# A decoder layer on one core: chunk-wise loading of x, an unnormalised first feature that leaves PSUM at once, and the norm's root computed in one piece

## The chip, the cores and the metric

One Trainium2 chip; the program runs on one of its cores. Times are device microseconds of one execution of the program. A profiled execution is one execution taken with the hardware profiler; its span is the time from its first to its last recorded instruction.

## What is computed

One layer of a hybrid decoder in fp32 for 1,024 prompt tokens and 8 sample tokens (1,032 columns), model width 1,024. The token mix (sliding-window attention and a gated DeltaNet) is untouched by the change apart from the norm ahead of it. What matters here is the norm and the feed-forward part, which comes twice, and the norm at the end:

```python
def rmsnorm(x, g):
    y = x * lax.rsqrt(jnp.mean(x * x, axis=-1, keepdims=True) + EPS)
    return y * g

def swiglu(x, w_in, w_out):          # w_in: 1024 x 5632, w_out: 2816 x 1024
    gate, up = jnp.split(x @ w_in, 2, axis=-1)
    return (jax.nn.silu(gate) * up) @ w_out

x = x + 0.5 * swiglu(rmsnorm(x, ffn1_norm_g), ffn1_w_in, ffn1_w_out)
x = x + token_mix(rmsnorm(x, mix_norm_g), ...)
x = x + 0.5 * swiglu(rmsnorm(x, ffn2_norm_g), ffn2_w_in, ffn2_w_out)
y = rmsnorm(x, final_norm_g)
```

The norm is a factor for each token, so it may be applied before the product with `w_in` or behind it.

## The kernel before

**Layout.** x is held transposed: 8 tiles of 128 model rows, tokens along the free axis. In the feed-forward parts the 1,032 tokens are four chunks of 258 (`HW`), named by half p and place l in it (c = 2p + l). A block of x holds one chunk of one half of K (`kh`, four of the eight tiles: 128 x 1,032 numbers, 516 KB).

**Products.** fp32 operands are split into a rounded part `hi` and a rest `lo`; `mm3` (L318) makes three matmuls of each product: hi·hi (L321), hi·lo (L322), lo·hi (L323). Weights arrive as `r`, are cast by ScalarE to `phi` and split by VectorE to `plo`. Most of the feed-forward input product runs in a Strassen-like scheme (`ffn_in`, L651), with combined operands of weights (`wop`) and of x (`xhi`, `xlo`); these combine the two chunks of a half and both halves of K, and need x with its norm applied. They are built by `x_ops` (L441) on GpSimd, ScalarE and VectorE.

**The head.** So that TensorE has work before the norm is there, `ffn_head` (L614) makes the first features plainly: four in the first feed-forward part, three in the second (`HEAD`, L38). A feature is 128 of the 2,816 gate rows and the same up rows. It works on `xg` = x times the norm's gain only (`xghi` by ScalarE, `xglo` by VectorE; chunks in order, K tile by K tile, in the job `scale`, L1617). For each chunk, 24 matmuls go into a `ps` bank (gate) and 24 into an `mm` bank (up). There are five `ps` banks, in turn, and three `mm` banks. The result is evacuated by `evac` (L618): VectorE multiplies the gate bank by the row `rs` (the root, one for each token), ScalarE applies Silu, VectorE multiplies the up bank by `rs`, GpSimd multiplies the two, and SyncE stores 258 columns. An evacuation needs `rs` of its chunk; it waits in the list `due`, and `settle_rs` keeps at most two waiting for the first feature and one later.

**The norm.** `squares` (L771) squares the two blocks of a chunk on ScalarE, adds them on GpSimd and folds them twice on VectorE into `acc`. `rstd` (L360) sums over partitions with six narrow matmuls (L243), computes the root in twelve VectorE instructions on 86 x 6 numbers (`nv`, `rsqt`, `rsqy`), and then for each of its two chunks: three diagonal matrices (`ident` times a column of the root, in a temporary `t2`), three matmuls that broadcast them over partitions into a `ps` bank, and `use` (in `prepare`, L784): a ScalarE copy to `rs` and eight VectorE multiplications of x. The norms of the mix and of the end use `rstd` as well, with three chunks of 344 tokens, together or one by one.

**What sets the order.** TensorE executes in the order in which the program writes instructions (`ORDERED`, L43). Background jobs (the generators that are spawned: `scale`, `prepare`, weight casts, the norms) are advanced while the matmuls are written: each `yield` gives a planned time, in nanoseconds of TensorE work, by which the job is put off, `PAD` being 400. So a job's matmuls fall between those of the foreground. The order of VectorE, ScalarE, GpSimd and SyncE is set by a scheduler that simulates the engines; each engine then runs its list strictly in order. Buffers come from an arena of 44 slots; the temporaries `t2` have four buffers.

**The start.** `build` (L1594) loads the norm's gains, issues 12 warming matmuls on a tile of ones (L145), loads the first gate weights, then the four blocks of half 0 (by `kh`, then l), the first up weights, the four blocks of half 1 and the constants.

Of the kernel before, what the change touches and what calls it, by code (L numbers as in the profile page):

```python
# [13 lines left out]
AF = mybir.ActivationFunctionType  # L14
ALU = mybir.AluOpType
# [4 lines left out]
P = 128  # L20
D = 1024
# [22 lines left out]
ATT_GENS = 4  # L44
PAD = 400.0
KEEP = 2
WARM = 12
A_LIVE = 9
PAD_MERGE = 4000.0
DIRECT = 2  # L50
# [64 lines left out]
class Net:  # L115
# [244 lines left out]
    def rstd(self, acc, cs, use):  # L360
        nc = self.nc
        yield PAD
        m = 115 if cs[0][1] > HW else 86
        offs = [[c0, c0 + m, c0 + w - m] for c0, w in cs]
        n = 3 * len(cs)
        ps = self.pps()
        v = self.t("nv", [P, 12])
        for i, o in enumerate(sum(offs, [])):
            self.mmul(ps[:m, i:i + 1], acc[:, o:o + m], self.ones[:, 0:1])
        nc.vector.tensor_scalar(v[:m, :n], ps[:m, :n], 1.0 / D, EPS, ALU.mult, ALU.add)  # L370
        r = self.rsqrt(v[:m, :n])
        for j, (c0, w) in enumerate(cs):
            dgt = self.t2(3 * m)
            for i in range(3):
                nc.vector.tensor_scalar(dgt[:m, i * m:(i + 1) * m], self.ident[:m, :m], r[:, 3 * j + i:3 * j + i + 1], None, ALU.mult)
            yield PAD
            bcs = self.pps()
            for i, o in enumerate(offs[j]):
                self.mmul(bcs[:, o - c0:o - c0 + m], self.ones[:m, :], dgt[:m, i * m:(i + 1) * m])
            use(bcs, c0, w)  # L380

    def norm(self, x, gi, c0, w, acc, out):
        nc = self.nc
# [230 lines left out]
    def ffn_head(self, xg, rs, done, hd, head):  # L614

        nc = self.nc

        def evac(f, c, pg, pu):  # L618
            s = slice(c * HW, (c + 1) * HW)
            sg, h = self.t2(HW), self.t2(HW)  # L620
            nc.vector.tensor_tensor(sg, pg, rs[:, s], ALU.mult)
            nc.scalar.activation(sg, sg, AF.Silu)
            nc.vector.tensor_tensor(h, pu, rs[:, s], ALU.mult)
            nc.gpsimd.tensor_tensor(h, h, sg, ALU.mult)
            nc.sync.dma_start(hd[:, f, s], h)

        for f in range(head):
            ws = self.need_op(self.wops[f], 0)
            for c in range(4):
                p, l = divmod(c, 2)  # L630
                self.settle_rs(2)
                ps = self.pps()[:, :HW], self.pmm()[:, :HW]
                for o, (whi, wlo) in zip(ps, ws):
                    for k in range(KT):
                        while (k, c) not in xg["ready"]:
                            self.spin()
                        hi, lo = xg["t"][p][k // 4][l]
                        q, ks = slice(k % 4 * HW, (k % 4 + 1) * HW), slice(k * P, (k + 1) * P)
                        self.mm3(o, whi[:, ks], wlo[:, ks], hi[:, q], lo[:, q], k == 0, k == KT - 1)
                    if c == 3:  # L640
                        self.fr(whi, wlo)
                self.due.append((lambda p=p, l=l: (p, l) in done, partial(evac, f, c, *ps)))
                self.settle_rs(2 if f == 0 else 1)
                if f == head - 1:
                    self.fr(*xg["t"][p][0][l], *xg["t"][p][1][l])
                self.adv(2)
            self.wops[f].clear()
        self.settle_rs(0)
        self.fr(rs)

    def ffn_in(self, xT, hd, tail, head):  # L651
# [104 lines left out]
        self.split(hi, lo, raw, eng)  # L756
        return hi, lo

    def x_blocks(self, get, p):

        xs = []
        for kh in range(2):
            xs.append([])
            for l in range(2):
                b = self.bt([P, 4 * HW], s="x")
                c0 = (2 * p + l) * HW
                self.nc.sync.dma_start(b.rearrange("p (k c) -> p k c", k=4), get(kh, c0))
                xs[-1].append(b)
        return xs

    def squares(self, xs, acc):  # L771

        nc = self.nc
        for l in range(2):
            yield from self.need(2)
            a, b = self.bt([P, 4 * HW], s="sq"), self.bt([P, 4 * HW], s="sq")
            nc.scalar.activation(a, xs[0][l], AF.Square)
            nc.scalar.activation(b, xs[1][l], AF.Square)
            nc.gpsimd.tensor_tensor(a, a, b, ALU.add)
            nc.vector.tensor_tensor(a[:, :2 * HW], a[:, :2 * HW], a[:, 2 * HW:], ALU.add)  # L780
            nc.vector.tensor_tensor(acc[:, l * HW:(l + 1) * HW], a[:, :HW], a[:, HW:2 * HW], ALU.add)
            self.fr(a, b)

    def prepare(self, p, xs, acc, gi, out, rs, done, sq=None):  # L784

        nc = self.nc
        if sq is not None:
            while any((KT - 1, 2 * p + l) not in sq for l in range(2)):
                yield -300.0
            yield from self.squares(xs, acc)  # L790

        def use(bcs, c0, w):
            l = c0 // HW
            nc.scalar.copy(rs[:, (2 * p + l) * HW:(2 * p + l + 1) * HW], bcs[:, :w])
            done.add((p, l))
            for k in range(KT):
                y = xs[k // 4][l][:, k % 4 * HW:(k % 4 + 1) * HW]
                nc.vector.scalar_tensor_tensor(y, y, self.norm_g[:, gi, k:k + 1], bcs[:, :w], ALU.mult, ALU.mult)

        yield from self.rstd(acc, [(0, HW), (HW, HW)], use)  # L800
        self.fr(acc)
        for ok in self.x_ops([xs[0][0], xs[0][1], xs[1][0], xs[1][1]], 4 * HW, out):
            yield -300.0 if ok else -500.0
# [790 lines left out]
def build(tc, io):  # L1594
    with ExitStack() as ctx:
        ctx.enter_context(tc.manual_schedule(engines=ORDERED))
        n = Net(tc, ctx, io)
        nc = tc.nc
# [61 lines left out]
        xT = [[], []]  # L1660
# [98 lines left out]
```

## Time and profile before

| what | us |
|---|---|
| median of three runs | 2114.11 |
| lowest and highest of them | 2110.12 to 2117.31 |
| profiled execution | 2115.43 |
| its span | 2113.2 |
| TensorE busy in it | 2024.6 |
| mean granted TensorE clock | 0.973 of full |

The first feed-forward part's head lies in the first 142 us of the span, the second's between about 1375 and 1470; the final norm ends the span. In the rows of the profile an instruction that a helper records has the helper's line (L89 for VectorE, ScalarE and GpSimd, L102 for SyncE), so there one goes by tile names: `xghi`/`xglo` are the splits of x times gain, `phi`/`plo` those of weights, `sq` and `acc` the squares, `nv`, `rsqt`, `rsqy` the root, `t<-ident` a diagonal, `x<-x,c_norm_g,ps` the norm's multiplication, `t<-ps,rs` and `t<-mm,rs` the evacuation, `sw` the result of `ffn_in`. Lengths of neighbouring instructions of an engine overlap by a little, so a chain is better read from start to start. A granted clock of 0.50 means that matmuls stream at half speed.

### The profile page before, as it was taken

Reading aid. Unit: us, or ns where it says so; the run is one execution under the profiler, and the core shown is the slowest. Engines: PE = TensorE matmul, PEld = TensorE weight load, DVE = VectorE, ACT = ScalarE, POOL = GpSimd, SP = SyncE. Lnnn points to the kernel's source line nnn. Section 1 sums busy time; section 2 is a strip of 40 time slices with the busy share of each in tenths; the row PEclk is TensorE's granted clock in tenths of the full one; section 3 lists DMA queues with packets and bytes.
Section 4 is the critical chain, followed back from the end, with each engine's and each line's share of the span. In section 5 each row is a group of like instructions: output and inputs, shape, how many; then the busy total and the mean of one; then the engine's idle time right before and its main releaser. Section 6 shows DMA issues by size and latency. Waiting matters only on the chain.

```text
span 2113.2 us, 37138 instructions
## 1 busy us (share of the span) xinstructions
PE 2024.6 (96%) x15062; PEld 1963.6 (93%) x15062; DVE 1222.1 (58%) x2624; ACT 699.8 (33%) x1491; POOL 594.9 (28%) x517
## 2 busy tenths in 40 slices
PE   7799999999999999999999979999999999999997
PEld 6799999999999998787888869899999999999997
DVE  7755555555533544676977874685555555464335
ACT  5233333333211333545243332443333333331112
POOL 3354444341000131332211111245444444200003
PEclk7999999999999999999999979999999999999999
DMA  4112222227322221211212151221222222552112
GB/s 152 60 58 91 81 73 84 86 71 281 113 68 60 84 81 35 69 45 32 67 46 50 57 181 35 97 70 61 86 81 83 79 81 76 194 195 84 55 41 81
DMA packets 109771, 180.81 MB, mean 86 GB/s; under 512 B 35168, under 2 KB 63744, under 8 KB 109584
## 3 DMA queue, kind: packets, MB, share of 16 engines
q1 hardware_dynamic: 109568, 178.41, 26.6%
q8 instruction: 118, 1.93, 0.4%
q14 instruction: 53, 0.43, 0.1%
q0 software_dynamic: 32, 0.03, 0.0%
HBM read 135.60 MB, written 43.85 MB: 85 GB/s over the span
## 4 chain that ended last, share of the span: by engine, by line
PE 40%; DVE 8%; DMA 1%; issue 1%; SPq 1%; ACT 0%; POOL 0%; DVEq 0%; ACTq 0%; POOLq 0%
PE mm L321 6%; PE mm L322 6%; PE mm L323 6%; PE ps L528 4%; PE ps L530 4%; PE ps L529 4%; PE ps L243 3%; PE mm L528 2%; PE mm L530 2%; PE mm L529 2%; DVE conv L89 1%; DVE inv L89 1%; SPq L102 1%; DVE Tb L89 1%; DVE x L89 1%
## 5 line engine op out<-in xcount | busy, mean ns | idle before, releaser
L528 PE MATMUL ps<-xhi,wop 128*128 128x258 f32 x1480 | 421.0, 284 | 7.4 <-DVE sw L89 7.2
L530 PE MATMUL ps<-xhi,wop 128*128 128x258 f32 x1480 | 419.3, 283 | 0.0
L529 PE MATMUL ps<-xlo,wop 128*128 128x258 f32 x1480 | 419.3, 283 | 0.0
L321 PE MATMUL mm<-hhi,hi 128*128 128x344 f32 x1008 | 322.3, 320 | 0.0
L322 PE MATMUL mm<-hlo,hi 128*128 128x344 f32 x1008 | 322.3, 320 | 0.0
L323 PE MATMUL mm<-hhi,lo 128*128 128x344 f32 x1008 | 321.6, 319 | 0.0
L89 DVE TENSOR_TENSOR wop<-r,wop 128x512 fp32r<-128x512 f32 x185 | 158.5, 859 | 253.9 <-ACT wop L89 239.8
L528 PEld LDWEIGHTS ps<-xhi,wop 128*128 128x128 f32 x1480 | 280.9, 190 | 8.7 <-issue 7.2
L529 PEld LDWEIGHTS ps<-xlo,wop 128*128 128x128 f32 x1480 | 281.9, 191 | 0.0
L530 PEld LDWEIGHTS ps<-xhi,wop 128*128 128x128 f32 x1480 | 281.2, 190 | 0.0
L89 DVE SCALAR_TENSOR_TENSOR x<-mm,x 128x344 f32<-128x344 f32 x240 | 123.3, 515 | 220.0 <-PE mm L323 217.9
L89 ACT CAST hi<-raw 128x1024 fp32r<-128x1024 f32 (+1 forms) x78 | 76.7, 984 | 357.0 <-PE mm L322 327.0
L321 PEld LDWEIGHTS mm<-hhi,hi 128*128 128x128 f32 x1008 | 189.4, 188 | 0.3 <-DVE x L89 0.3
L323 PEld LDWEIGHTS mm<-hhi,lo 128*128 128x128 f32 x1008 | 189.4, 188 | 0.0
L322 PEld LDWEIGHTS mm<-hlo,hi 128*128 128x128 f32 x1008 | 189.3, 188 | 0.0
L89 POOL TENSOR_TENSOR acc<-acc,t 128x344 f32<-128x344 f32 (+1 forms) x50 | 45.5, 911 | 508.2 <-ACT t L89 495.9
L321 PE MATMUL mm<-xnhi,hi 128*128 128x344 f32 x488 | 172.1, 353 | 0.0
L528 PE MATMUL mm<-xhi,wop 128*128 128x258 f32 x592 | 167.5, 283 | 0.0
L530 PE MATMUL mm<-xhi,wop 128*128 128x258 f32 x592 | 167.2, 283 | 0.0
L529 PE MATMUL mm<-xlo,wop 128*128 128x258 f32 x592 | 167.0, 282 | 0.0
L89 ACT CAST wop<-r 128x512 fp32r<-128x512 f32 x185 | 114.7, 621 | 144.6 <-PE mm L530 77.0
L323 PE MATMUL mm<-xnhi,lo 128*128 128x344 f32 x488 | 158.6, 325 | 0.0
(320 smaller groups left out, 4607.5 us busy)
## 6 DMA issues: line engine op xcount, KB each, us to landing
r<-in_w_in SPq DMA_DIRECT2D x86, 512.0 KB, 3.6
hraw<-hd SPq DMA_DIRECT2D x44, 516.0 KB, 5.0
hd<-sw SPq DMA_DIRECT2D x74, 258.0 KB, 2.0
raw<-in_w_out SPq DMA_DIRECT2D x34, 512.0 KB, 4.0
raw<-in_w_mix SPq DMA_DIRECT2D x22, 512.0 KB, 3.6
raw<-in_w_out SPq DMA_DIRECT2D x24, 384.0 KB, 3.2
x<-in_x SPq DMA_DIRECT2D x16, 516.0 KB, 9.0
xd<-x SPq DMA_DIRECT2D x24, 172.0 KB, 1.9
```

Of the source, the lines that this page charges most:

```text
L89: return fn(out, *a, **k)
L102: return self.eng.dma_start(out, src)
L243: self.nc.tensor.matmul(out, lhsT, rhs, start=start, stop=stop)
L321: mm(ps, whi, xhi, start=start, stop=False)
L322: mm(ps, whi, xlo, start=False, stop=False)
L323: mm(ps, wlo, xhi, start=False, stop=stop)
L528: mm(ps, w[:, a], x[0][:, c], start=first, stop=False, skip_group_check=True)
L529: mm(ps, w[:, a], x[1][:, c], start=False, stop=False, skip_group_check=True)
L530: mm(ps, wlo, x[0][:, c], start=False, stop=last, skip_group_check=True)
```

## The change

- There are 18 warming matmuls in place of 12.
- x is loaded chunk by chunk in half 0: both blocks of chunk 0, then the up weights, then both blocks of chunk 1, then half 1.
- The addition of two squared blocks runs on VectorE in half 0 of the first head; in half 1 it stays on GpSimd.
- Feature 0 of a head no longer waits for the root: two ScalarE copies for each chunk take gate and up from PSUM into two tiles `early` of 1,032 columns. When all four chunks of `rs` are there, a job multiplies both tiles by `rs` on VectorE, applies Silu on ScalarE, multiplies on GpSimd and stores the feature with one DMA in place of four. `settle_rs` keeps one evacuation waiting in the other features, as before.
- In `rstd`, the root and the first chunk's diagonals are emitted at high priority; then the job yields 2,500 (`PAD_B`) in place of 400 before the first broadcast. The diagonals of the next chunk are emitted at high priority right behind the broadcast of the one before, into a tile `dgt` that has a single buffer, and a yield of 400 follows each `use`. Both heads, the norm of the mix and that at the end are affected.

TensorE's list has the same length otherwise, and its matmuls the same shapes.

```diff
-WARM = 12
+WARM = 18
+PAD_B = 2500.0
...
-        nc.vector.tensor_scalar(v[:m, :n], ps[:m, :n], 1.0 / D, EPS, ALU.mult, ALU.add)
-        r = self.rsqrt(v[:m, :n])
+
+        def diag(j):
+            d = self.t("dgt", [P, 345], bufs=1)[:, :3 * m]
+            for i in range(3):
+                nc.vector.tensor_scalar(d[:m, i * m:(i + 1) * m], self.ident[:m, :m], r[:, 3 * j + i:3 * j + i + 1], None, ALU.mult)
+            dgts.append(d)
+
+        dgts = []
+        with self.tc.high_priority():
+            nc.vector.tensor_scalar(v[:m, :n], ps[:m, :n], 1.0 / D, EPS, ALU.mult, ALU.add)
+            r = self.rsqrt(v[:m, :n])
+            diag(0)
+        yield PAD_B
         for j, (c0, w) in enumerate(cs):
-            dgt = self.t2(3 * m)
-            for i in range(3):
-                nc.vector.tensor_scalar(dgt[:m, i * m:(i + 1) * m], self.ident[:m, :m], r[:, 3 * j + i:3 * j + i + 1], None, ALU.mult)
-            yield PAD
+            dgt = dgts[j]
             bcs = self.pps()
             for i, o in enumerate(offs[j]):
                 self.mmul(bcs[:, o - c0:o - c0 + m], self.ones[:m, :], dgt[:m, i * m:(i + 1) * m])
+            if j + 1 < len(cs):
+                with self.tc.high_priority():
+                    diag(j + 1)
             use(bcs, c0, w)
+            yield PAD
...
+        def first():
+            while len(done) < 4:
+                yield -300.0
+            for t in early:
+                nc.vector.tensor_tensor(t, t, rs, ALU.mult)
+            nc.scalar.activation(early[0], early[0], AF.Silu)
+            nc.gpsimd.tensor_tensor(early[1], early[1], early[0], ALU.mult)
+            nc.sync.dma_start(hd[:, 0, :], early[1])
+            self.fr(*early)
+            yield PAD
+
+        early = [self.bt(s="early") for _ in range(2)]
         for f in range(head):
...
-                self.due.append((lambda p=p, l=l: (p, l) in done, partial(evac, f, c, *ps)))
-                self.settle_rs(2 if f == 0 else 1)
+                if f:
+                    self.due.append((lambda p=p, l=l: (p, l) in done, partial(evac, f, c, *ps)))
+                    self.settle_rs(1)
+                else:
+                    for t, o in zip(early, ps):
+                        nc.scalar.copy(t[:, c * HW:(c + 1) * HW], o)
...
+            if f == 0:
+                late = self.spawn(first())
             self.wops[f].clear()
         self.settle_rs(0)
+        self.wait(late)
         self.fr(rs)
...
-    def x_blocks(self, get, p):
-
-        xs = []
-        for kh in range(2):
-            xs.append([])
-            for l in range(2):
+    def x_blocks(self, get, p, xs=None, ls=(0, 1)):
+
+        xs = [[], []] if xs is None else xs
+        for l in ls:
+            for kh in range(2):
...
-            nc.gpsimd.tensor_tensor(a, a, b, ALU.add)
+            eng.tensor_tensor(a, a, b, ALU.add)
...
-        xs = [n.x_blocks(src(io["x"]), 0)]
+        xs = [n.x_blocks(src(io["x"]), 0, None, (0,))]
         n.adv()
+        n.x_blocks(src(io["x"]), 0, xs[0], (1,))
         xs.append(n.x_blocks(src(io["x"]), 1))
...
-            n.spawn(n.prepare(p, xs[p], n.bt(s="acc"), 0, xT[p], rs, done, xg["ready"]))
+            n.spawn(n.prepare(p, xs[p], n.bt(s="acc"), 0, xT[p], rs, done, xg["ready"], (n.nc.vector, n.nc.gpsimd)[p]))
```

More of the change, by code (lines that the diff above doesn't have):

```diff
@@ L767, in x_blocks, with squares @@
                 self.nc.sync.dma_start(b.rearrange("p (k c) -> p k c", k=4), get(kh, c0))
-                xs[-1].append(b)
+                xs[kh].append(b)
         return xs
-    def squares(self, xs, acc):
+    def squares(self, xs, acc, eng):
         nc = self.nc
@@ L782, in squares, with prepare @@
             self.fr(a, b)
-    def prepare(self, p, xs, acc, gi, out, rs, done, sq=None):
+    def prepare(self, p, xs, acc, gi, out, rs, done, sq=None, eng=None):
         nc = self.nc
@@ L789, in prepare @@
                 yield -300.0
-            yield from self.squares(xs, acc)
+            yield from self.squares(xs, acc, eng)
         def use(bcs, c0, w):
```

## The prediction

> **What bounds the kernel now.** The first part of the page says which engine fills the span.
>
> ```profile
> PE 2024.6 (96%) x15062; PEld 1963.6 (93%) x15062; DVE 1222.1 (58%) x2624; ACT 699.8 (33%) x1491; POOL 594.9 (28%) x517
> ```
>
> TensorE is idle for only 2113.2 - 2024.6 = 88.6 us, so a change that leaves the products alone, as this one does, can win only idle time and time at a low clock. Where these lie is read from the table by stretches; after the stretch and its length stand busy time and count of PE, PEld, DVE, ACT and POOL, then the granted clock, DMA share and GB/s.
>
> ```profile
> 0.00:20.00 20.00, 11.79 (x50) 10.22 (x50) 10.36 (x18) 14.48 (x28) 5.23 (x9) 0.69 0.89 287
> 20.00:40.00 20.00, 16.69 (x123) 16.69 (x123) 17.69 (x33) 11.89 (x22) 10.13 (x3) 0.80 0.31 107
> 40.00:60.00 20.00, 14.35 (x106) 14.04 (x105) 16.54 (x52) 5.50 (x8) 4.41 (x3) 0.83 0.11 34
> 60.00:80.00 20.00, 11.59 (x67) 11.50 (x68) 19.83 (x31) 6.25 (x10) 11.11 (x5) 0.74 0.13 39
> 80.00:120.00 40.00, 40.00 (x336) 40.00 (x335) 14.09 (x26) 7.46 (x13) 8.23 (x9) 1.00 0.23 68
> 120.00:160.00 40.00, 36.84 (x293) 36.46 (x292) 25.37 (x31) 16.04 (x26) 27.11 (x18) 0.96 0.20 63
> 900.00:1100.00 200.00, 190.82 (x1377) 168.73 (x1376) 151.18 (x458) 92.62 (x276) 46.76 (x45) 0.95 0.18 47
> 1100.00:1300.00 200.00, 177.46 (x1370) 165.31 (x1369) 146.73 (x504) 69.35 (x194) 31.70 (x15) 0.92 0.29 84
> ```
>
> The first 80 us hold 25.6 us of idle TensorE (8.21 + 3.31 + 5.65 + 8.41) and a clock of 0.69 to 0.83; from 80 on it is full: 336 products in 40 us, 0.119 us each. This is the head that the change rewrites. The DeltaNet stage (900 to 1300) idles 31.7 us and is not the target. The longest waits of TensorE in the first 150 us say for whom (sum, times, longest):
>
> ```profile
> PE mm L321 <- DVE t L89: 7.8, 1, 7.8
> PE ps L321 <- ACT xghi L89: 5.1, 2, 3.2
> PE ps L321 <- DVE x L89: 3.5, 1, 3.5
> PE mm L323 <- DVE plo L89: 3.4, 1, 3.4
> PE ps L528 <- DVE sw L89: 3.0, 1, 3.0
> ```
>
> The timeline of TensorE gives the places (start, length, instruction, idle before and releaser).
>
> ```profile
> 8.75 0.58 PE L321 MATMUL ps<-xghi,phi 128*128 128x258 f32 x1 [3.21 <-ACT xghi L89]
> 23.31 0.58 PE L323 MATMUL mm<-xghi,plo 128*128 128x258 f32 x1 [3.43 <-DVE plo L89]
> 43.53 1.55 PE L243 MATMUL ps<-t,ones 86*128 86x86 f32 x6 [2.81 <-DVE t L89]
> 53.44 0.80 PE L243 MATMUL ps<-t,ones 86*128 86x86 f32 x6
> 64.91 0.55 PE L321 MATMUL mm<-xghi,phi 128*128 128x258 f32 x1 [7.76 <-DVE t L89]
> 74.77 0.36 PE L321 MATMUL ps<-xghi,phi 128*128 128x258 f32 x1 [3.49 <-DVE x L89]
> 93.64 0.28 PE L321 MATMUL ps<-xghi,phi 128*128 128x258 f32 x1
> ```
>
> Feature 0 (8 groups of 24 products) runs from 8.75 to 53.4, feature 1 from there to 93.64, where feature 2 starts; behind that TensorE stays full but for one 3.0 us wait, so time won before 93.64 is carried to the end.
>
> **Feature 0: loads, early evacuation, squares.** The SyncE queue at the start (x are blocks of tokens, r raw weights: the first r is the gate, the second the up half), before and then after:
>
> ```order
> L102 DMA r_2_91<-in_w_in1 128x512 x2
> L102 DMA x_5_100<-in_x 128x4x258
> L102 DMA x_6_102<-in_x 128x4x258
> L102 DMA x_7_104<-in_x 128x4x258
> L102 DMA x_8_106<-in_x 128x4x258
> L102 DMA r_9_108<-in_w_in1 128x512 x2
> ```
> ```order
> L103 DMA r_2_97<-in_w_in1 128x512 x2
> L103 DMA x_5_106<-in_x 128x4x258
> L103 DMA x_6_108<-in_x 128x4x258
> L103 DMA r_7_110<-in_w_in1 128x512 x2
> L103 DMA x_10_119<-in_x 128x4x258
> L103 DMA x_11_121<-in_x 128x4x258
> ```
>
> The up weights pass two blocks of x, and the second block is now the other half of chunk 0, not the first half of chunk 1. ScalarE casts in that order; its rows, and VectorE's and GpSimd's beside them:
>
> ```profile
> 8.18 1.71 ACT L89 ACTIVATE xghi<-x,c_norm_g 128x258 fp32r<-128x258 f32 x4 [2.74 <-DMA x<-in_x]
> 9.80 1.05 ACT L89 ACTIVATE sq<-x 128x1032 f32<-128x1032 f32 x1
> 18.43 1.12 ACT L89 CAST phi<-r 128x512 fp32r<-128x512 f32 x2
> 45.12 0.38 ACT L89 COPY rs<-ps 128x258 f32<-128x258 f32 x1 [8.90 <-PE ps L243]
> ```
> ```profile
> 16.40 5.65 DVE L89 SCALAR_TENSOR_TENSOR xglo<-x,c_norm_g,xghi 128x258 fp32r<-128x258 f32 x4 [0.87 <-ACT xghi L89]
> 22.57 0.68 DVE L89 TENSOR_TENSOR plo<-r,phi 128x512 fp32r<-128x512 f32 x1
> ```
> ```profile
> 16.05 2.39 POOL L89 TENSOR_TENSOR sq<-sq,sq 128x1032 f32<-128x1032 f32 x1 [13.63 <-ACT sq L89]
> 18.60 2.37 POOL L89 TENSOR_TENSOR sq<-sq,sq 128x1032 f32<-128x1032 f32 x1 [0.17 <-ACT sq L89]
> ```
>
> Start to start, a block takes ScalarE 9.80 - 8.18 = 1.62 us, so neighbours overlap by 0.09; a square counts 0.95, a cast of half a weight tile 0.56, a copy 0.34. The order after the change, from 8.18: block 9.8, square 10.75, block 12.4, square 13.3, two casts 14.4. So chunk 0's gate products end near 14.2 and, with two splits of 0.68 on VectorE, its up products can start at 15.8 instead of 19.1 to 23.3. At half clock they end at 20.9, at full clock at 18.7. From 14.4 ScalarE goes on with chunk 1 (two blocks, two squares, one copy: 19.9, its second block done at 19.0), chunk 2 (second block 24.1), chunk 3 (27.7): TensorE follows by one chunk, gate of c3 done at 31.0, the norm's sums 32.0, c3's up products (24 x 0.119 = 2.9) at 34.9. It was 53.4: **-18.4 us**, the largest term. The eight copies cost 8 x 0.34 = 2.7 us of ScalarE, counted in; each waits for products that are done when it comes up, so nothing behind it is held.
>
> The two adds of squares that go from GpSimd to VectorE: VectorE's group of four splits took 5.65 us where GpSimd added (16.05 to 20.97). The adds on VectorE I count at 1.2 us each, twice the 0.6 of a 512-column split, which is less than the 5.65 shows lost to GpSimd.
>
> The six extra warming products end near 7.8 us and leave about 1 us idle where 3.2 stood. I do not count on a full clock (the 48 products of 8.75 to 28.0 all ran at 0.50), since c1 waits for ScalarE anyway; it is worth at most 1.5 us, in the low end.
>
> **Feature 1: broadcasts and the root.** Old cost: 93.6 - 53.4 = 40.2. VectorE and GpSimd at its largest wait (57 to 65):
>
> ```profile
> 41.35 0.16 DVE L89 TENSOR_TENSOR rsqt<-rsqy 86x6 f32<-86x6 f32 x1
> 59.17 2.23 DVE L89 SCALAR_TENSOR_TENSOR rsqy<-rsqt,rsqy 86x6 f32<-86x6 f32 x1
> 61.43 2.67 DVE L89 TENSOR_SCALAR t<-ident,rsqy 86x86 f32<-86x86 f32 x3
> 71.39 3.23 DVE L89 SCALAR_TENSOR_TENSOR x<-x,c_norm_g,ps 128x258 f32<-128x258 f32 x8
> ```
> ```profile
> 59.00 2.37 POOL L89 TENSOR_TENSOR t<-x,t 128x1032 f32<-128x1032 f32 x1
> 61.34 2.35 POOL L89 TENSOR_TENSOR x<-x,x 128x1032 f32<-128x1032 f32 x1
> ```
>
> A 6-column step of the root, 0.16 us alone, took 2.23 us and ended with the GpSimd add beside it, while the x multiplications, which read PSUM, ran at 3.23 / 8. The Trainium skill, "SBUF — State Buffer", section "Who interferes with whom", says the same: a VectorE instruction with two SBUF inputs waits out a GpSimd instruction that reads SBUF, one with a single SBUF input does not. By it each such root step can cost up to one GpSimd add; if nothing were waited out, the wait below would be 2.8 us shorter.
>
> The places of root and diagonal on VectorE (t2 or dgt from ident are the diagonals of a chunk's root, the x rows its normalisation), before:
>
> ```order
> L89 SCALAR_TENSOR_TENSOR x_8_106<-x_8_106,c_norm_g_74,ps_71_561 128x258 x4
> L89 TENSOR_TENSOR rsqt_69_539<-rsqy_68_538 86x6
> L89 SCALAR_TENSOR_TENSOR rsqt_69_539<-rsqt_69_539,nv_67_530 86x6
> L89 SCALAR_TENSOR_TENSOR rsqy_68_538<-rsqt_69_539,rsqy_68_538 86x6
> L89 TENSOR_SCALAR t2_70_551<-ident_125,rsqy_68_538 86x86 x3
> ```
>
> and after:
>
> ```order
> L90 SCALAR_TENSOR_TENSOR x_11_121<-x_11_121,c_norm_g_74,ps_85_706 128x258 x4
> L90 TENSOR_TENSOR t2_88_769<-ps_72_589,rs_32_184 128x258
> L90 TENSOR_TENSOR t2_89_770<-mm_73_590,rs_32_184 128x258
> L90 SCALAR_TENSOR_TENSOR rsqy_78_644<-rsqt_79_645,rsqy_78_644 86x6
> L90 TENSOR_TENSOR rsqt_79_645<-rsqy_78_644 86x6
> L90 SCALAR_TENSOR_TENSOR rsqt_79_645<-rsqt_79_645,nv_77_636 86x6
> L90 SCALAR_TENSOR_TENSOR rsqy_78_644<-rsqt_79_645,rsqy_78_644 86x6
> L90 TENSOR_SCALAR dgt_80_657<-ident_131,rsqy_78_644 86x86 x3
> ```
>
> The second half's root is still cut by x multiplications, at high priority too, and two evacuations now stand in it.
>
> First half: sums at 32, twelve steps among splits of weights and square adds (0.2 each start to start, and 4.7 us of others) put the first diagonal at 39.9; TensorE reaches its broadcast, 54 products on, at 41.7: no wait, where 2.81 stood. The second diagonal stands right behind the first on VectorE and, with one buffer, waits for that broadcast. Behind it are queued the split of feature 2's up weights (which land near 43 anyway) and chunk 0's x multiplications; they start about 45 and end at 48.5, before chunk 1's broadcast at about 50 needs their bank. Cost 0, cover about 1 us.
>
> Second half: TensorE is at chunk 2's broadcast at 53.6. The multiplications of chunk 1 run 50.5 to 53.9, the two evacuations to 54.5, and the root's four steps and the diagonal need 1.4 more undisturbed; with the rest of one add, 57.4 at best. With two or three adds of 2.37 beside them (chunk 1's x releases three, as before) it is 60.2; at worst 62.5. I take 60.2, since the same steps met the same adds before: a wait of 6.7, in place of 7.76 + 3.49. So feature 1 costs 192 x 0.119 = 22.9, four broadcasts and sums 2.9, the wait 6.7, and half clock behind it, 2.0:
>
> ```profile
> 64.90:69.00 4.10, 4.09 (x19) 0.50 0.10 34
> ```
>
> (19 products in 4.09 where 2.27 would do). Together 34.5, so feature 2 starts at 69.4 and not 93.64: feature 1 gives **-5.8**, both **-24.2**. The clock fell to half at 43.5 after an idle of 2.81 us. The Trainium skill, "TensorE: Matmul & The Clock Gate", Part 1, puts the fall behind an idle window of about 3.4 us; no such minimum is seen here, so the row decides and a wait of 3 us is charged with 2 us too; by the page the better case below would be 2 us lower.
>
> The late job (two VectorE multiplications at about 1.2, one Silu, one GpSimd product of 2.4, one store for four) runs after 69 beside full products: 0.
>
> **The second head, the mix, the tail.** The second FFN's head has x at hand and waits only for roots:
>
> ```profile
> 1379.70 0.90 PE L243 MATMUL ps<-t,ones 86*128 86x86 f32 x6 [1.56 <-DVE t L89]
> 1398.71 0.68 PE L243 MATMUL ps<-t,ones 86*128 86x86 f32 x4 [1.15 <-DVE t L89]
> 1401.18 0.73 PE L243 MATMUL ps<-t,ones 86*128 86x86 f32 x2 [1.80 <-DVE t L89]
> ```
>
> That is 4.5 us, and with 3 us of half clock 7.5 that may go. The first broadcast stands 21 products (2.5 us) later, more than its wait; the others are of the second half, as above, and may stay. **-4**, bounds 0 and -7.5. In the mix the broadcasts go 12 products later, which I take at 0 (at most 2 us). In the tail the chain of the last chunk (sums, root, broadcast, multiplication, store) is the same; the broadcast of the chunk before moves 12 products on,
>
> ```profile
> 2089.69 0.82 PE L243 MATMUL ps<-t,ones 115*128 115x115 f32 x6
> ```
>
> to 2091.6, so its multiplications come nearer to the last evacuations: **+0.3**, an estimate, at most 0.6.
>
> Sum: -24.2 - 4 + 0.3 = -27.9 on the profiled execution's 2115.4, 2087.5. The median of the runs is 1.3 below that execution: **2086**.
>
> **The rivals.**
> - *Better*: GpSimd's adds miss the root (57.4: -2.8), the second head's waits all go (-3.5): 2080. For it, priority and the later broadcasts; against, the order above. 0.14.
> - *The up weights come late*. ScalarE is strictly in order, and the weights' cast now stands ahead of chunk 1. The DMA engines ran full to about 19 us (share 0.89 in the first 20). If the queued x blocks share them with the weights, these land at 18 and not 13.4: +4.6, 2091. Against: x's first block landed at 8.1 with all others queued behind it. 0.12.
> - *A wait at the start of the Strassen products*. The 3.0 us wait for sw stands after the last of the first four features; the second half's operands are built there, beside 27.11 us of GpSimd in 40. The margin from the last x multiplication to it shrinks by about 14 us and 2.4 us of GpSimd come in. If the builds move behind it, the wait grows by 8: 2094. 0.10.
> - *Slower*: the scheduler also moves VectorE rows in the DeltaNet stage (root steps, convolutions, z and S updates change places). TensorE waits 31.7 us there, on VectorE above all. If each chain there meets one more instruction and these waits double, +32: 2118. From +22 on the change is no change, from +34 it is slower. For it: waits there of 4 us each; against: the moves are by a few rows and go both ways. 0.12: half of it between the two points, half beyond.
>
> The forecast itself has 0.52, for 2086 and its own bounds of 2079 to 2092.
>
> **How the numbers follow.** The low end takes the full wait of chunk 2 at its best (-2.8), the second head (-3.5), the clock (-1.5): 2078, rounded to 2077. The high end takes in the late weights and the wait at the Strassen products with a worst root (+2.3, second head +4): 2101. What a measurement can tell here is 0.3%, 6 us. Faster: 0.52 + 0.14 + 0.12 + 0.10 = 0.88; same 0.06; slower 0.06.
>
> **What would show it.** Right: feature 2's first product near 69 us; one wait of 4 to 9 us in the first 80, at chunk 2's broadcast, released by the diagonal; none for plo, xghi beyond chunk 1 or x. Wrong: a cast of up weights that waits for its DMA; feature 0 still under way at 40; a wait of over 6 us for sw; DeltaNet's idle above 40 us.

## The result

The changed kernel takes 2094.76 us in the median (2093.44 to 2096.83, four runs), the kernel before 2115.71 us in the runs beside it (2110.12 to 2117.38): a ratio of 0.9904, with a 95% interval of 0.9881 to 0.9928. Timed again on another occasion it took 2092.34 against 2113.06, ratio 0.990 (0.988 to 0.992). The gain of about 21 us has the forecast's sign; the forecast point was 2086, a gain of 28. The time lies in the whole range, 2077 to 2101, but above the forecast's own bounds of 2079 to 2092: the high end had been drawn for late weights, a longer wait for `sw`, a worse root and a second head that wins nothing, and of these only the longer wait for the root came.

### The profile page after: what moved, and what is told of

It reads as the page before. It is cut to its first block, busy times and chain, and to the rows that moved or that the text cites. A ratio compares the mean times of both kernels' runs of the same rounds, so it can differ in the third digit from the quotient of the medians.

```text
span 2091.7 us, 37132 instructions
## 1 busy us (share of the span) xinstructions
PE 2018.9 (97%) x15074; PEld 1957.6 (94%) x15074; DVE 1214.5 (58%) x2614; ACT 703.4 (34%) x1501; POOL 586.8 (28%) x509
## 4 chain that ended last, share of the span: by engine, by line
PE 80%; DVE 11%; DMA 3%; ACT 2%; issue 2%; SPq 1%; POOL 1%; DVEq 0%; ACTq 0%; POOLq 0%
PE mm L322 12%; PE mm L323 12%; PE mm L324 12%; PE ps L541 8%; PE ps L543 8%; PE ps L542 8%; PE ps L244 6%; PE mm L541 3%; PE mm L542 3%; PE mm L543 3%; DVE conv L90 1%; DMA r<-in_w_in 1%; PE ps L322 1%; PE ps L324 1%; PE ps L323 1%
## 5 line engine op out<-in xcount | busy, mean ns | idle before, releaser
L323 PE MATMUL mm<-xnlo,hi 128*128 128x344 f32 x488 | 158.8, 325 | 0.0
```

What stands on the lines that cost most here:

```text
L323: mm(ps, whi, xlo, start=False, stop=False)
```

## The profile after

The table by stretches, for the stretches of before:

```profile
0.00:20.00 20.00, 17.03 (x109) 16.02 (x110) 12.63 (x26) 15.51 (x31) 1.45 (x7) 1.00 0.90 288
20.00:40.00 20.00, 20.00 (x173) 20.00 (x172) 15.77 (x37) 13.97 (x29) 4.94 (x2) 1.00 0.40 133
40.00:60.00 20.00, 14.48 (x124) 14.10 (x123) 15.81 (x44) 5.81 (x8) 5.09 (x4) 0.94 0.20 61
60.00:80.00 20.00, 15.88 (x118) 15.88 (x119) 18.62 (x32) 6.70 (x9) 8.83 (x4) 0.80 0.13 40
80.00:120.00 40.00, 40.00 (x335) 40.00 (x334) 25.32 (x30) 14.34 (x23) 25.87 (x16) 1.00 0.19 64
```

The first 40 us hold 3 us of idle time, at full clock; what else is idle lies between 40 and 80. The waits of TensorE in the first 150 us put it into one instruction:

```profile
PE ps L244 <- DVE dgt L90: 9.0, 1, 9.0
PE ps L541 <- DVE sw L90: 3.5, 1, 3.5
PE ps L146 <- DVE ones L90: 1.1, 1, 1.1
PE mm L324 <- DVE plo L90: 0.9, 1, 0.9
PE ps L244 <- DVE x L90: 0.6, 1, 0.6
```

And TensorE's timeline has it at the broadcast of chunk 2 (the first row is feature 1's first product, the last feature 2's):

```profile
35.27 0.28 PE L322 MATMUL ps<-xghi,phi 128*128 128x258 f32 x1
...
50.93 0.87 PE L244 MATMUL ps<-dgt,ones 86*128 86x86 f32 x6 [0.60 <-DVE x L90]
...
64.12 1.58 PE L244 MATMUL ps<-dgt,ones 86*128 86x86 f32 x6 [9.04 <-DVE dgt L90]
...
73.71 0.36 PE L322 MATMUL ps<-xghi,phi 128*128 128x258 f32 x1
```

Feature 0 ends at 35.3 instead of 53.4, feature 2 starts at 73.7 instead of 93.6: 19.9 us, nearly the whole difference. (1.0 of it is no work of the change: x's first block, which stands at the same place of the queue, landed earlier in this profile, and the first product started at 7.72 instead of 8.75.) Followed from one landmark of TensorE's order to the next, the lead of the changed kernel in the two profiles is 19.2 us behind the first Strassen products, about 18 us before and behind the DeltaNet stage (and between 11 and 18 within it), 21.4 at the Strassen products of the second feed-forward part and 21.5 at the end of the span. So the second head brings 3.3 us, the tail nothing, and the stages between cost about 1.

What holds chunk 2's broadcast is seen on VectorE, whose list is late from 46.41 on, since the split of feature 2's up weights waits for ScalarE's cast, and that for its DMA:

```profile
45.33 1.05 ACT L90 CAST phi<-r 128x1024 fp32r<-128x1024 f32 x1 [8.60 <-DMA r<-in_w_in]
```
```profile
46.41 1.23 DVE L90 TENSOR_TENSOR plo<-r,phi 128x1024 fp32r<-128x1024 f32 x1 [2.85 <-ACT phi L90]
...
51.44 1.22 DVE L90 TENSOR_TENSOR xlo<-x,xhi 128x1032 fp32r<-128x1032 f32 x1
52.58 0.72 DVE L90 TENSOR_SCALAR rsqt<-nv 86x6 int32<-86x6 int32 x1
...
54.21 1.26 DVE L90 SCALAR_TENSOR_TENSOR x<-x,c_norm_g,ps 128x258 f32<-128x258 f32 x3
...
55.47 2.05 DVE L90 SCALAR_TENSOR_TENSOR x<-x,c_norm_g,ps 128x258 f32<-128x258 f32 x5
...
59.17 2.28 DVE L90 SCALAR_TENSOR_TENSOR rsqt<-rsqt,nv 86x6 f32<-86x6 f32 x1
61.49 2.28 DVE L90 SCALAR_TENSOR_TENSOR rsqy<-rsqt,rsqy 86x6 f32<-86x6 f32 x1
63.80 0.61 DVE L90 TENSOR_SCALAR dgt<-ident,rsqy 86x86 f32<-86x86 f32 x3
```

and on GpSimd:

```profile
56.07 2.36 POOL L90 TENSOR_TENSOR t<-x,x 128x1032 f32<-128x1032 f32 x1 [2.79 <-DVE x L90]
58.39 0.73 POOL L90 TENSOR_TENSOR t<-t,t 128x258 f32<-128x258 f32 x1
59.08 2.36 POOL L90 TENSOR_TENSOR t<-x,t 128x1032 f32<-128x1032 f32 x1
61.39 2.36 POOL L90 TENSOR_TENSOR x<-x,x 128x1032 f32<-128x1032 f32 x1
```

Two steps on 86 x 6 numbers last 2.28 us each and end when the GpSimd additions do (61.44 and 63.75).

## The experiments

Each kernel is the changed one with one edit; only the last two, which say so, have several. A single time of one run says little here: kernels whose TensorE order is the same in the DeltaNet stage differ by several us there (last section). So the verdicts on the head go by its landmarks: the end of feature 0 (35.3 in the changed kernel) and the start of feature 2 (73.7). The first product started between 7.1 and 9.5 us in the profiles, as x arrived, which is told where it matters. In three runs (old root, squares on GpSimd, the last version) the last of the four broadcasts, 0.6 us of TensorE, stands behind feature 2's start and not ahead of it, so 0.6 of their lead at that landmark is not won.

### Without the early evacuation

```diff
...
-                if f:
-                    self.due.append((lambda p=p, l=l: (p, l) in done, partial(evac, f, c, *ps)))
-                    self.settle_rs(1)
-                else:
-                    for t, o in zip(early, ps):
-                        nc.scalar.copy(t[:, c * HW:(c + 1) * HW], o)
+                self.due.append((lambda p=p, l=l: (p, l) in done, partial(evac, f, c, *ps)))
+                self.settle_rs(2 if f == 0 else 1)
...
```

> Only the early evacuation is undone: feature 0 is evacuated as before the change, with the root, two evacuations waiting. Theory (the forecast's): this is the part that carries the gain of feature 0, since there are three up banks and the fourth chunk's up products must wait until chunk 0 is evacuated, that is for the first root. The first diagonal stands at about 41 us, so a wait of 6 to 9 us comes back ahead of chunk 3, feature 0 ends near 46 instead of 35.3, and feature 2 starts 5 to 10 us later than with the whole change (73.7), at 79 to 84; time about 2100 to 2105. Rival (loads, clock and root carry the gain, the banks would do): feature 2 starts within 2 us of 73.7.

It took 2113.51 us in one run, beside one of 2112.64 of the kernel before: the whole gain was gone. TensorE's waits and feature 2's first product:

```profile
PE ps L244 <- DVE dgt L90: 13.3, 3, 6.9
```
```profile
90.16 0.28 PE L322 MATMUL ps<-xghi,phi 128*128 128x258 f32 x1
```

Feature 0 ends near 52, feature 2 starts 16.5 us later than with the whole change, more than expected: there are three waits for a diagonal, in two broadcasts, 6.9 us in the first. As x came late here (first product at 9.45, 1.7 later than in the changed kernel), 14.7 of the 16.5 us are the edit's. The rival, that loads, clock and root would do without it, is out. Of the 19.9 us in the head, about 15 need this part.

### The old order of the loads

```diff
-        for l in ls:
-            for kh in range(2):
+        for kh in range(2):
+            for l in ls:
...
-        xs = [n.x_blocks(src(io["x"]), 0, None, (0,))]
+        xs = [n.x_blocks(src(io["x"]), 0)]
         n.adv()
-        n.x_blocks(src(io["x"]), 0, xs[0], (1,))
```

> Only the order of the loads is undone: all four blocks of half 0, then the up weights. Theory: the up weights are cast behind the fourth block, near 18 us instead of 12.3, so TensorE idles about 4 us more ahead of chunk 0's up products and runs at half clock for some us behind it; feature 0 ends 4 to 8 us later than 35.3, feature 2 starts at 77 to 81. Rival (ScalarE paces feature 0 as a whole, so its order does not matter): feature 0 ends within 1 us of 35.3.

TensorE's timeline (the first row is the end of feature 0, the last the start of feature 2):

```profile
43.19 0.28 PE L322 MATMUL ps<-xghi,phi 128*128 128x258 f32 x1
...
63.73 0.68 PE L244 MATMUL ps<-dgt,ones 86*128 86x86 f32 x4 [1.58 <-DVE dgt L90]
66.19 0.73 PE L244 MATMUL ps<-dgt,ones 86*128 86x86 f32 x2 [1.78 <-DVE dgt L90]
...
74.95 0.36 PE L322 MATMUL ps<-xghi,phi 128*128 128x258 f32 x1
```

Feature 0 ends 7.9 us later, as the theory had it. But feature 2 starts only 1.2 us later: where the changed kernel waits 9.0 us for the second half's root, this one waits 3.4. TensorE comes later to a root that hardly moves. The new order of the loads wins 8 us and gives back nearly seven. The single time was 2087.53, below the changed kernel's, so it was timed:

> The old order of the loads again, timed. Theory (the 8 us that the new order wins in feature 0 are given back at the second half's root, whose chain does not run through TensorE; the single time of 2087.5 was a DeltaNet stage with a full clock): median within 3 us of the changed kernel's, at most 2 us above. Rival (the old order is truly better, by something behind the head): 5 to 8 us below the changed kernel in the median.

Median 2093.63 (2087.86 to 2102.34, six runs) beside 2092.34 of the changed kernel in the same session (ratios to before 0.9909, 0.9886 to 0.9932, and 0.990, 0.988 to 0.992): no difference that can be measured. The rival is not supported.

### Twelve warming products

> Only the warming products are undone, 12 instead of 18. Theory after seeing the changed profile, in which TensorE was busy without a gap from 14.3 to 40 us at full clock: the clock falls to half behind the idle time after the 12th product and chunk 0 runs at half clock, so that feature 0 ends 2 to 4 us later than 35.3. The forecast's own claim (chunk 1 waits for ScalarE anyway): at most 1.5 us later. A rival in which the clock rises by itself: no difference.

Only the constant is edited. The first product came at 8.55 and not 7.72, and feature 0 ended at 36.11: 27.56 us from one to the other, 27.55 with 18. Feature 2 started at 75.8. The clock, from the stretch behind the first product, 12 warming products first and then 18:

```profile
8.00:17.00 9.00, 7.45 (x41) 0.81 1.08 358
```
```profile
8.00:17.00 9.00, 7.09 (x48) 1.00 1.08 357
```

So six more products keep the clock full, but feature 0 is not shorter for it: chunk 0's slower products fill time in which its inputs are still being made. The forecast's "at most 1.5 us" stands for feature 0, the expectation of 2 to 4 falls. Feature 2 comes 67.2 us behind the first product, and 66.0 with 18; behind the 9.1 us wait at the broadcast the clock was 0.50 over 5 us here and 0.61 there. The time of the run, 2097.58, is a single one.

### The old root

```diff
...
-        with self.tc.high_priority():
-            nc.vector.tensor_scalar(v[:m, :n], ps[:m, :n], 1.0 / D, EPS, ALU.mult, ALU.add)
-            r = self.rsqrt(v[:m, :n])
-            diag(0)
-        yield PAD_B
+        nc.vector.tensor_scalar(v[:m, :n], ps[:m, :n], 1.0 / D, EPS, ALU.mult, ALU.add)
+        r = self.rsqrt(v[:m, :n])
         for j, (c0, w) in enumerate(cs):
+            dgt = self.t2(3 * m)
+            for i in range(3):
+                nc.vector.tensor_scalar(dgt[:m, i * m:(i + 1) * m], self.ident[:m, :m], r[:, 3 * j + i:3 * j + i + 1], None, ALU.mult)
+            yield PAD
...
```

> Only the norm's routine is undone: the root and the diagonals in temporaries, at normal priority, 400 ns before each broadcast; early evacuation, loads, clock and squares stay. Theory: the first broadcast stands 21 products earlier and so waits 2 to 4 us for the root, and the second half's broadcasts wait 6 to 10 us as with the change; feature 2 starts 1 to 5 us later than 73.7, and the second head loses its 4 us again: time about 2098 to 2104. Rival (the root in one piece is what removes the second half's wait, too): a wait of over 12 us for the second half. Rival on the other side (the later broadcasts cost more than they save): feature 2 starts earlier than 73.7.

2095.45 us in one run. In the first head the waits are 1.9 us at the first broadcast and 6.7 at a later one, and feature 2 starts at 72.3, 1.4 us earlier than with the new root: there, the root in one piece wins nothing, and the expectation (1 to 5 later) was wrong; what came is the sign of the rival that the later broadcasts cost more than they save. In the second head it does win. The waits for a diagonal there, old root and then new:

```profile
PE ps L244 <- DVE t L90: 6.3, 3, 2.6
```
```profile
PE ps L244 <- DVE dgt L90: 1.0, 1, 1.0
```

Between the end of the DeltaNet stage and the second Strassen products this kernel loses 7 us against the changed one: it loses 3.9 against the kernel before, where the changed one wins 3.1. So in these single profiles the early evacuation with the old root is a loss in the second head, and the new root brings the whole gain there.

### Squares of half 0 on GpSimd

> Only the place of the additions of squares is undone: half 0's two additions run on GpSimd again. Theory (as forecast): VectorE's splits of x beside them stretch, 1 to 4 us in all, so chunk 1 and chunk 2 come later and feature 0 ends 1 to 3 us later than 35.3. But as the run with the old loads has shown that feature 0's end is given back at the second half's root, feature 2 should start within 1.5 us of 73.7 all the same. Rival: VectorE gets 2.4 us of work off its list, the first root comes earlier and feature 2 starts earlier than 73.

```diff
-... rs, done, xg["ready"], (n.nc.vector, n.nc.gpsimd)[p]))
+... rs, done, xg["ready"], n.nc.gpsimd))
```

One run, 2090.24 us. Feature 0 ends at 38.3, its first product being at 7.99, so 2.7 us later. VectorE's two splits of the up weights, with GpSimd's addition in front of them:

```profile
13.19 3.06 DVE L90 TENSOR_TENSOR plo<-r,phi 128x512 fp32r<-128x512 f32 x2 [0.97 <-ACT phi L90]
```
```profile
12.74 2.37 POOL L90 TENSOR_TENSOR sq<-sq,sq 128x1032 f32<-128x1032 f32 x1 [10.33 <-ACT sq L90]
```

They take 3.06 us; the changed kernel's took 1.29. Yet feature 2 starts at 72.3, within the 1.5 us expected, and the wait at the second half's root is 5.8 instead of 9.0: this loss, too, is given back there. The rival's landmark (earlier than 73) came as well, but not by its reason: the first diagonal starts at 43.49, 2.2 us later than in the changed kernel.

### What the second half's root waits for

Two causes stand in the profile: GpSimd's additions beside the root's steps, and the multiplications of chunk 1, which came late to VectorE because the split of feature 2's up weights stood ahead of chunk 0's and waited for its DMA (cast at 45.33). First the additions alone:

```diff
...
+        if behind is not None:
+            self.nc.gpsimd.tensor_copy(t1[:, 0:1], behind)
         tt(t1, b12, b11, ALU.subtract)
...
```

Here `behind` is one column of chunk 2's row of roots.

> The changed kernel, but GpSimd's first difference for half 0's operands is made to wait for the broadcast of chunk 2 (a one-column copy from its row of roots is written into the result first), so that no GpSimd addition of 1,032 columns runs beside the second half's root. Theory 1 (GpSimd holds up the root's small steps, which took 2.28 us instead of 0.2): the four steps and the diagonal end at about 59.5 instead of 64.3, the wait ahead of chunk 2's broadcast falls from 9.0 to 4 to 5 us, feature 2 starts at about 69. Theory 2 (the steps are late because multiplications and evacuations stand ahead of them on VectorE; GpSimd only fills that time): the wait stays at 8 or more. Against both a possible return of the time: half 0's operands are built later, and the wait for the Strassen products grows by up to 5 us.

VectorE, and GpSimd's first addition:

```profile
58.07 0.16 DVE L90 SCALAR_TENSOR_TENSOR rsqy<-rsqt,rsqy 86x6 f32<-86x6 f32 x1
58.26 0.16 DVE L90 TENSOR_TENSOR rsqt<-rsqy 86x6 f32<-86x6 f32 x1
58.46 0.64 DVE L90 SCALAR_TENSOR_TENSOR rsqt<-rsqt,nv 86x6 f32<-86x6 f32 x1
59.13 0.16 DVE L90 SCALAR_TENSOR_TENSOR rsqy<-rsqt,rsqy 86x6 f32<-86x6 f32 x1
59.33 0.61 DVE L90 TENSOR_SCALAR dgt<-ident,rsqy 86x86 f32<-86x86 f32 x3
```
```profile
62.00 2.40 POOL L90 TENSOR_TENSOR t<-x,x 128x1032 f32<-128x1032 f32 x1
```

VectorE's order and times are those of the changed kernel up to 58.1. The same steps at the same place then take 0.16 to 0.64 us (the 0.64 beside a GpSimd instruction of 0.73), the wait is 4.6, feature 2 starts at 69.8, 3.9 us earlier. GpSimd's additions cost 4.4 us of the 9.0: shown. The Trainium skill, "SBUF — State Buffer", section "Who interferes with whom", says that a VectorE instruction with two SBUF inputs contends with a GpSimd instruction that reads SBUF; the trace agrees (2.28 us beside an addition of 2.36, at most 0.64 without it). The time:

> The kernel in which GpSimd's additions wait for chunk 2's broadcast, timed. Theory: the 3.9 us that feature 2 starts earlier and no larger wait for the Strassen products (3.7 against 3.5) give 3 to 4 us less than the changed kernel in the median: 2090 to 2092. Rival (given back later): within 1 us of it.

Single run 2089.86; timed 2088.12 (2086.83 to 2094.36, six runs) beside 2092.34. The difference of 4.2 agrees with the head's 4, though the slowest of the six runs is as long as the slowest of the changed kernel; the wait for `sw` was 4.0 and 3.7.

Then the up weights alone:

```diff
...
         for src in (s1, s2):
+            while behind is not None and src is s2 and behind not in self.seen:
+                yield False
...
+            if behind is not None and src is s2:
+                self.nc.scalar.copy(hi[:, 0:1], self.rs0)
...
```

Here `rs0` is one column of chunk 0's row of roots.

> The changed kernel, but the cast of feature 2's up weights is put behind the first row of roots (a one-column copy), so that their split no longer stands ahead of chunk 0's multiplications on VectorE, where it waited 2.9 us for its DMA. Allocation moves chunk 1's and chunk 2's broadcasts 6 products forward. Theory 2 (order on VectorE): the multiplications start at 43.5 instead of 47.6, the root's chain runs 2 to 4 us earlier, feature 2 starts at about 70 to 71. Theory 1 alone (GpSimd): the additions simply meet the steps again, the wait stays at 8 to 9 us and feature 2 starts within 1 us of 73.7.

```profile
43.26 3.23 DVE L90 SCALAR_TENSOR_TENSOR x<-x,c_norm_g,ps 128x258 f32<-128x258 f32 x8
...
55.50 2.28 DVE L90 SCALAR_TENSOR_TENSOR rsqt<-rsqt,nv 86x6 f32<-86x6 f32 x1
57.82 2.29 DVE L90 SCALAR_TENSOR_TENSOR rsqy<-rsqt,rsqy 86x6 f32<-86x6 f32 x1
...
61.76 0.60 DVE L90 TENSOR_SCALAR dgt<-ident,rsqy 86x86 f32<-86x86 f32 x3
```

Chunk 0's multiplications start 4.3 us earlier, but the diagonal is only 2.0 earlier: GpSimd blocks two steps as before, and three more steps of the root and a split of x (1.22) stand between these and the diagonal. The broadcasts moved 6 products forward as well. Wait 8.7, feature 2 at 72.3 (first product at 7.12, 0.6 earlier than in the changed kernel), time 2090.75 in one run. So order alone is worth a us or less while GpSimd adds beside it. Both edits together:

> Both edits together. If both causes are real and add: second diagonal at 55 to 57 us, a wait of 2 to 3 us ahead of chunk 2's broadcast, feature 2 at 65 to 67 instead of 73.7, and about 7 us off the time if nothing gives it back; the wait for the Strassen products (3.5 us) may grow by up to 5. If one of the causes is none: as the other edit alone.

Wait 3.2, feature 2 at 68.7, with x arriving 1.7 us later than in the changed kernel (first product at 9.44). Measured from the first product, feature 2 comes after 59.3 us, against 66.0 (changed), 65.2 (up weights) and about 62 (additions): together they bring 6.7 us, more than the 0.8 and 4.1 of each alone. The diagonal (58.2) and the wait (3.2) came a little later and longer than the 55 to 57 and 2 to 3 expected. The landmark was later than the 65 to 67 expected by that late x. One run, 2090.44 us.

Last, a version of both with the second half's broadcasts put off by 30 more products:

```diff
...
-        yield from self.rstd(acc, [(0, HW), (HW, HW)], use)
+        yield from self.rstd(acc, [(0, HW), (HW, HW)], use, 6000.0 if sq is not None and p else PAD_B)
...
```

> A version made of what the runs showed: GpSimd's additions behind chunk 2's broadcast, feature 2's up weights behind chunk 0's roots, and the second half's broadcasts put off by 6,000 instead of 2,500, that is 30 products (3.6 us) later on TensorE, so that the remaining wait of 3.2 us is covered by products. Theory: no wait over 1 us in the first 100 us, no half clock behind one, feature 2 at 63 to 66 us, 8 to 10 us less than the changed kernel: 2085 to 2088. Rival (the later broadcasts hold the evacuations and with them the banks and the operands of the Strassen products): the wait for sw grows beyond 7 us and the time stays above 2089.

```profile
PE ps L543 <- DVE sw L90: 2.4, 1, 2.4
PE ps L322 <- ACT xghi L90: 2.1, 2, 1.8
PE ps L322 <- ACT phi L90: 1.7, 1, 1.7
PE ps L146 <- DVE ones L90: 1.1, 1, 1.1
```
```profile
62.87 0.28 PE L322 MATMUL ps<-xghi,phi 128*128 128x258 f32 x1
```

No broadcast waits any more; feature 2 starts at 62.9. (Against the expectation, waits of 1.8 and 1.7 us are left in the first 100: one for x at the start, one for feature 3's weights.) Median 2084.22 us (2083.53 to 2084.52, four runs), 8.1 below the changed kernel's in the same session and 0.9861 (0.9839 to 0.9882) of the kernel before: the fastest here. Feature 2 starts 11.4 us earlier than in the changed kernel's profile of that session (74.23); some 4 us go again by the first Strassen products, most of them near 90 us, where feature 3's weights are now the late ones (the wait for phi, 1.7, one for plo, 0.8, and a low clock behind).

The unaltered changed kernel ran beside these:

> The changed kernel unaltered, timed beside the next three on one chip. Both theories: 2093 to 2097 us, feature 2 near 73.7 us. It also shows how far the DeltaNet stage (900 to 1100 us) moves between executions of the same program: in the earlier profiles of kernels that are identical there, that stage differed by up to 9 us with the granted clock.

2092.34 (2090.47 to 2094.25, five runs), feature 2 at 74.2, 9.1 us of wait: the head repeats to 0.5 us in two profiles.

## Why the prediction was right, and where it missed

- **Feature 0, -18.4 us: right, with some luck.** It ended at 35.3, forecast 34.9. Luck is 1.0 us of it: ScalarE's first block started at 7.15, where the working took 8.18 from the profile before, because x landed earlier. The reason given was half right. ScalarE, and VectorE's split of the up weights, set the pace up to 14 us; from there TensorE is full to 40 us at full clock, which the forecast had not counted on, so it is products, 24 in 2.87 us, that set the end.
- **Who brings it.** The working put the gain on order of loads and early evacuation together. The runs part them: without the evacuation about 15 us are lost at feature 2, without the new loads 1.2 and nothing measurable in time.
- **First half's root, no wait: right** (broadcast at 42.1, forecast 41.7). **Chunk 1's broadcast with a cover of about 1 us:** it waited 0.6.
- **Chunk 2's wait of 6.7 us: right in kind, too small.** It was 9.0, the largest miss. The step that failed is "the multiplications of chunk 1 run 50.5 to 53.9": they ran 54.2 to 57.5, because a split of x and the root's first steps stood between, and those came late because the split of feature 2's up weights had waited ahead of them (46.4 instead of about 44): the working had these weights land near 43, and they were cast at 45.33. From there the working holds: from the end of the evacuations to the end of the diagonal 6.2 us where it had 5.7, two steps blocked by GpSimd for 2.28 each. Feature 2 started 4.3 us later than forecast: 0.4 from feature 0, 0.6 at chunk 1's broadcast, 2.3 at this wait, and 1.0 of matmuls, as TensorE is busy for 28.8 us between the two features where the working had 27.8. The half clock behind the wait (26 matmuls in the 4.9 us from 64 to 69, six of them the broadcast) was foreseen with 2.0 us.
- **GpSimd against VectorE: right, by rows that show less than was read from them.** The x multiplications at 71.39 had no GpSimd instruction beside them (GpSimd is idle from 70.4 to 75.8); the row that does bear it out is the changed kernel's 55.47, five in 2.05 us beside the addition at 56.07. And it does not hold that one SBUF input makes an instruction safe: the three diagonals, a matrix times a column of the root, took 0.61 us alone, 2.67 beside the addition of 61.34 in the kernel before, and 3.25 beside additions in the run with the old loads.
- **The clock.** The idle time of 2.81 us at 43.5 came right behind twelve one-column matmuls (0.9 us), so that row alone does not show that so short an idle costs the clock; the last section has rows that do. The better case leaves a wait of 3.9 us, longer than the 3.4 that the working quotes, so it would not be 2 us lower by that figure.
- **What the sum did not see:** feature 0's end and the second half's root are not terms that add. The root's chain runs through ScalarE, VectorE and GpSimd and hardly moves with TensorE, so time won before it turns into waiting at it. The runs with the old loads and with the squares on GpSimd show this directly: 7.9 and 2.7 us lost in feature 0, 1.2 later and 1.4 earlier at feature 2.
- **The second head, -4: right,** -3.3 measured; the run with the old root shows the new one at work there (7 us).
- **The late job: 0, right:** TensorE is full from 80 to 120. **The tail, +0.3:** nothing seen. **The wait for sw** went from 3.0 to 3.5; the rival that it grows by 8 did not come.
- **Late up weights** (a rival): the cast of the up weights did not wait for its DMA; it ran at 12.29, behind the square.
- **The DeltaNet stage** (the slower rival): idle there 29.1 us (200 - 192.78 and 200 - 178.10) against 31.7. Not supported.
- **The signs.** Feature 2 was to start near 69: it started at 73.7. One wait of 4 to 9 us at chunk 2's broadcast, released by the diagonal: it came, at 9.0. No wait for `plo` or x: one of 0.9 and one of 0.6 came. Of the four signs of being wrong none came as it was meant, but a cast of up weights did wait for its DMA, that of feature 2 at 45.33, and it had its part in the miss at chunk 2.
- **Slips in the working,** none of which changes the forecast by more than 0.4 us: 53.4 - 34.9 is 18.5 and not 18.4, 60.2 - 53.6 is 6.6 and not 6.7, and 41.7 for the first broadcast is 57 products behind 34.9 (as TensorE's list has it), not 54.
- The sum was 27.9 and the measured gain 21: 4.3 us are missing in the first head, 0.7 in the second, 0.8 at the first Strassen products and the tail, and about 1 in stages whose clock varies.

## What to carry to other kernels

A wait at a chain that does not run through the busy engine can swallow what is won ahead of it, as 7 of 8 us here; before summing gains, ask for each wait whether its releaser would come earlier too. A step of a root on 86 x 6 numbers, 0.16 us alone, took up to 2.28 us here beside a GpSimd addition of 2.36, so put GpSimd's large additions outside a latency chain, if need be by a false dependency of one column. And an in-order engine's early prefetch work (here a split that waits for its DMA) belongs behind the chain, not ahead of it.

## What was not expected of the hardware

The same stretch of the DeltaNet stage ran at different granted clocks in profiles whose TensorE order is the same there (VectorE and ScalarE have one instruction each at another place). The changed kernel, and then the one with the old loads, 910 to 930 us:

```profile
910.00:920.00 10.00, 8.73 (x28) 0.66 0.05 13
920.00:930.00 10.00, 10.00 (x65) 0.83 0.01 2
```
```profile
910.00:920.00 10.00, 8.47 (x50) 1.00 0.05 13
920.00:930.00 10.00, 10.00 (x87) 1.00 0.17 43
```

In both TensorE waited at 911, for 2.2 and 1.7 us; in one the clock fell, in the other it did not, and by 936 the first had lost 7 us against the second. The program alone does not decide it, for the second profile of the unaltered changed kernel waited 1.1 us there and kept the clock. The two profiles of the same program:

```profile
911.27 1.97 PE L244 MATMUL ps<-S,vtok 128*64 128x256 f32 x4 [2.23 <-ACT S L90]
```
```profile
912.76 1.08 PE L244 MATMUL ps<-S,vtok 128*64 128x256 f32 x4 [1.08 <-ACT S L90]
```

Thirteen of the fourteen profiles show this wait, and its length parts them: behind the six of 2.02 to 2.65 us the clock was 0.50 to 0.66 over the next 5 us, behind the seven of 0.19 to 1.75 us it was 1.00. But no one length holds at other places: a wait of 3.47 us for `sw` at 129 in the kernel with the old loads left the clock at 1.00, and one of 1.64 us at 968 in the changed kernel was followed by 0.66. What else decides is open. That the clock moves so is the likely reason, though not shown, why one run of a kernel here spreads over several us (the kernel before: 2106.5 to 2120.0 in eleven runs); it is why landmarks ahead of that stage were the better measure.
